# Long convolutions and their filters by a transform folded in time and in frequency, on eight shared 128x128 blocks

## The chip, the cores and the metric

One core of a Trainium2 chip runs the whole program. The metric is the device time of one execution in microseconds (us), as the median of several runs; lower is better. The core has five engines with a queue of instructions each: TensorE (PE, matrix products; its weight loads are listed as PEld), VectorE (DVE), ScalarE (ACT), GpSimd (POOL) and SyncE (SP), which here only issues transfers. An engine takes its instructions in order and waits on semaphores of the others.

## The reference

Two encoder layers on x of 512 times and 1024 channels. Each layer norms x, multiplies by one wide matrix `w_in`, and feeds two branches: differential attention with four heads, and a Hyena branch. In the Hyena branch three streams of 512 channels go through a short convolution of three taps. Then come two long convolutions, each with its own filter of 512 forward and 511 backward taps that a small network computes from the position, and each followed by a product with a gate:

```python
z = fft_long_conv(hv, filt[:, 0], flt_bias[l, 0]) * hx1
z = fft_long_conv(z, filt[:, 1], flt_bias[l, 1]) * hx2
y_h = z * silu(z_h)
def fft_long_conv(u, h_f, bias):            # n = 1024, cut to the first 512 times
    return irfft(rfft(u, n=2 * L) * h_f, n=2 * L)[:, :L] + u * bias
```

Both branches are gated by sigmoids, projected by `w_pa` and `w_ph`, added, projected by `w_out`, normed and added to x. All of it is float32.

## The kernel before, in words

Every float32 product is made of three: each operand is split into a high and a low part (`split`: a copy on ScalarE gives hi, a subtraction on VectorE gives lo), and `mm3` (line 180) accumulates hi*hi, hi*lo and lo*hi. The weights come through three buffers `wraw`, 256 KB a load, each split into `whi` and `wlo`.

The transform of 1024 points is cut into four groups of frequencies. `conv_in` turns a stream so that time is on the partition, adds and subtracts the four tiles of 128 times, and splits eight inputs. `conv_group` (one call for each of four groups) makes the real and imaginary part of a group from two inputs, 12 products 256 wide in all, multiplies by the filter's spectrum H that is read from DRAM, and splits the result. `conv_out` (one call for each of two tiles of 128 channels) goes back to time with the data as the stationary operand, 24 products 256 wide a call, so that its result has the channel on the partition, undoes the additions, and multiplies by the gate. A layer has four such convolutions: two filters (o) by two halves of 256 channels (hc). The filters themselves go through the same forward blocks in `filter_group`, eight calls for each of the eight filters of the program; the spectra are stored to DRAM.

The four constant tables `fh`, `fl`, `ih`, `il` hold 13 blocks of 128x128 each and are loaded by GpSimd's queue early in the program.

The order of the program is written as lists of steps that `mix` spreads evenly over each other, and a scheduler orders each engine's queue from it; `ahead(n)` lets a method's instructions rank n places earlier. In `layer`, after the attention, there are three such mixes around the long convolutions: the first convolution of half 0 with the rest of the Hyena projections, the first convolution of half 1 with three steps of `merge_a` (the gate and projection of the attention branch, 36 products 512 wide each), and the second convolution of both halves with the other five steps of `merge_a`. Then come eight steps of `merge_h`, in layer 0 mixed with three filters of layer 1, and the output projection. The eight `merge_a` steps of a layer each end in one instruction on VectorE at line 797, so these mark the stretch of the convolutions in the trace.

Of the kernel before, what the change touches and what calls it, by code (L numbers as in the profile page):

```python
# [17 lines left out]
P = 128  # L18
# [5 lines left out]
# tiles of each tag: how many, values a partition  # L24
TILES = {"hT": (8, 1024), "ya": (8, 512), "yh": (4, 1024), "s1": (12, 512), "s2": (4, 1024), "u": (12, 512),
         "ld": (2, 1024), "wraw": (3, 512), "whi": (4, 512), "wlo": (4, 512), "za": (2, 512), "a": (4, 512), "b": (3, 512)}
C8 = math.sqrt(0.5)
# [11 lines left out]
# ---------------------------------------------------------------- constants of the shapes  # L39
# [9 lines left out]

def _dft_matrices():  # L50
    p = np.arange(P, dtype=np.float64)[:, None]
    k = np.arange(P, dtype=np.float64)[None, :]
    th = 2 * np.pi * ((4 * k * p) % NF) / NF
    ph = [2 * np.pi * (((8 * k + r) * p) % NF) / NF for r in range(4)]
    sg = 1.0 - 2.0 * (k % 2)
    ny = (1.0 - 2.0 * (p % 2)) * np.ones((1, P))
    c, s = np.cos, np.sin

    def nyq(m):
        m = m.copy()  # L60
        m[:, 0] = ny[:, 0]
        return m

    fw = [c(th), sg * c(th), nyq(-s(th)), nyq(-sg * s(th)),
          c(ph[2]), -s(ph[2]), -c(ph[2]),
          c(ph[1]), -s(ph[1]), -c(ph[1]),
          c(ph[3]), s(ph[3]), -s(ph[3])]
    fw = np.stack(fw, 1)

    w = 2.0 / NF  # L70
    thT, sgT = th.T, sg.T
    e_re = w * c(thT)
    o_re = w * sgT * c(thT)
    e_im = -w * s(thT)
    o_im = -w * sgT * s(thT)
    e_re[0] = o_re[0] = 1.0 / NF
    e_im[0] = o_im[0] = ny[:, 0] / NF

    iv = [e_re, o_re, e_im, o_im, w * c(ph[2].T), -w * s(ph[2].T), -w * c(ph[2].T)]
    for r in (1, 3):  # L80
        iv += [-w * s(ph[r].T), w * c(ph[r].T), w * s(ph[r].T)]
    iv = np.stack(iv, 1)
    return fw, iv


def _constants():
    out = {}
    fw, iv = _dft_matrices()
    out["c_fh"], out["c_fl"] = _hi_lo(fw)
    out["c_ih"], out["c_il"] = _hi_lo(iv)  # L90
# [11 lines left out]
    ang = ((f32(2 * math.pi) * i[:, None]) * f[None, :] / f32(S)).astype(np.float64)  # L102
    out["c_z"] = np.ascontiguousarray(
        np.concatenate([t[None, :].astype(np.float64), np.cos(ang).T, -np.sin(ang).T], 0).astype(f32))
    p = np.arange(P)[:, None]
    out["c_nt"] = np.ascontiguousarray(
        np.concatenate([-t.reshape(4, P).T, np.where(p == 0, -1e30, 0.0), p > 0], 1).astype(f32))
    return out


# blocks of the forward matrices: per group the (re, im) pairs for its two inputs
FW = (((0, 1), (2, 3)), ((4, 5), (5, 6)), ((7, 8), (8, 9)), ((10, 11), (12, 10)))
# first of the two adjacent blocks of the inverse matrices for re and im
IV = ((0, 2), (4, 5), (8, 7), (11, 10))
# inputs of the groups among the slots [g, e, d, s, a1, b1, a3, b3]
SLOTS = ((1, 3), (0, 2), (4, 5), (6, 7))
# [14 lines left out]
def ahead(n):  # L131
    """the scheduler ranks the instructions of the method n places before (after, if negative) their place in the program"""
# [8 lines left out]
# ---------------------------------------------------------------- the kernel  # L141
class Net:
# [9 lines left out]
    # ---- tiles: the tiles of one tag are given out in the order of the program, so each stream has its own  # L152
    def t(self, tag, dt=F32, a=None):
        t = self.pools[tag].tile([P, TILES[tag][1]], dt, name=tag, tag=tag)
        return t if a is None else t.rearrange("p (a c) -> p a c", a=a)

# [10 lines left out]
    # ---- pieces  # L167
# [6 lines left out]
    def mm3(self, out, pairs):  # L174
        """out = sum of lhs.T @ rhs in float32, each operand given as (hi, lo)"""
# [6 lines left out]

    def split(self, hi, lo, src):
# [3 lines left out]
    def weights(self, src, to=None):  # L187
        """src: [128 k, c] of a matrix in DRAM, 512 values a partition -> (hi, lo), each [128, k, c]"""
# [8 lines left out]
    def rstd(self, ss, n, mul, eps, tag):  # L197
        """(ss * mul + eps) ** -0.5 of [128, n]"""
# [7 lines left out]
    def gain(self, src):  # L206
        g = [self.t("s1") for _ in range(2)]
# [4 lines left out]
    # ---- constants  # L212
# [9 lines left out]
    def load_dft(self):  # L222
        nc, a = self.nc, self.a
        self.fh = self.const([P, 13, P], "fh", F32R)
        self.fl = self.const([P, 13, P], "fl", F32R)
        self.ih = self.const([P, 13, P], "ih", F32R)
        self.il = self.const([P, 13, P], "il", F32R)
        for t, n in ((self.fh, "c_fh"), (self.fl, "c_fl"), (self.ih, "c_ih"), (self.il, "c_il")):
            self.tc.keep_in_program_order(nc.gpsimd.dma_start(out=t, in_=a[n]))

    def vectors(self):
        """the vectors over channels, channel on the partition: one transpose for each layer"""
        nc, a = self.nc, self.a
        self.nt = self.const([P, 6], "nt")
# [16 lines left out]
    def lambdas(self):  # L251
        """-lam of each layer, on every partition"""
# [22 lines left out]
    def bias_table(self):  # L275
        """tab[h, j] = -bias of head h at relative position j - 512"""
# [34 lines left out]
    def filter_mlp(self):  # L311
# [15 lines left out]
        # (hi, lo) of one layer, or (lo, hi), stacked along the contraction  # L327
# [10 lines left out]
        self.H = [[self.dram.tile([P, 2, 9, 256], F32, name=f"H{l}{o}", tag=f"H{l}{o}") for o in range(2)]  # L338
                  for l in range(DEPTH)]

    def filter_steps(self, l, blocks, where):
        """steps that fill H[l]; where: the phase that they run in, which has its own tiles to spare"""
        steps, late = [], []

        def group(*args):
            """the products of a group follow the splits of the next"""
            self.filter_split(*args[-3:])
            late.append(args)
            if len(late) > 1:
                self.filter_group(*late.pop(0))  # L350

        for o, hc in blocks:
            st = {"where": where}
            steps.append(lambda o=o, hc=hc, st=st: self.filter_load(l, o, hc, st))
            steps += [lambda o=o, t=t, st=st: self.filter_taps(l, t, st) for t in range(4)]
            for im in range(2):
                steps.append(lambda im=im, st=st: self.filter_sums(l, im, st))
                steps += [lambda o=o, hc=hc, im=im, g=g, st=st: group(l, o, hc, im, g, st) for g in range(4)]
        if blocks:
            steps.append(lambda: self.filter_group(*late.pop(0)))  # L360
        return steps

    def two(self, st):
        """two [128, 2, 256]"""
# [24 lines left out]
    def filter_taps(self, l, t, st):  # L389
        """sum and difference of the two directions at the times of tile t"""  # L390
# [6 lines left out]
        if t:  # L397
            nc.scalar.activation(out=h, in_=st["dl"], func=AF.Exp, scale=self.nt[:, t:t + 1])
        else:
            # the backward taps have none at time 0  # L400
            for d in range(2):
                nc.scalar.activation(out=h[:, d], in_=st["dl"][:, d], func=AF.Exp, scale=self.nt[:, 0:1],
                                     bias=self.nt[:, 4:5] if d else 0.0)
        nc.vector.tensor_tensor(out=h, in0=ps, in1=h, op=ALU.mult)
        if t == 0:
# [4 lines left out]
    def filter_sums(self, l, im, st):  # L410
        """st["T"][im] = (x0, x1), (x2, x3) -> (e, s), (g, d)"""
        x = st["T"][im]
        st["y"] = self.two(st)
        for y, op in zip(st["y"], (ALU.add, ALU.subtract)):
            self.nc.vector.tensor_tensor(out=y, in0=x[0], in1=x[1], op=op)

    @ahead(60)
    def filter_split(self, im, g, st):
        """the inputs of group g"""
        nc = self.nc  # L420
        es, gd = st["y"]
        if g < 2:
            src = (es, gd)[g]
        else:
            src = self.t("b", a=2)
            for j, y in enumerate((gd, es)):
                nc.vector.scalar_tensor_tensor(out=src[:, j], in0=y[:, 1], scalar=(C8 if g == 2 else -C8),
                                               in1=st["T"][im][j][:, 0], op0=ALU.mult, op1=ALU.add)
# [5 lines left out]
        self.split(yh, yl, src)  # L434
        st["in", im, g] = yh, yl

    def filter_group(self, l, o, hc, im, g, st):
        nc = self.nc
        yh, yl = st.pop(("in", im, g))
        ps = self.ps("po", 2)  # L440
        m = FW[g][im]
# [553 lines left out]
```

## Time and profile before

| what | value |
|---|---|
| time, median of 3 runs | 1008.47 us (1007.25 to 1008.93) |
| profiled execution: span | 1008.5 us |
| PE busy | 974.7 us (97%), 5619 matmuls |
| PEld busy | 847.6 us (84%) |
| DVE busy | 763.2 us (76%), 1599 instructions |
| ACT busy | 505.8 us (50%), 1035 instructions |
| POOL busy | 32.7 us (3%) |
| moved by DMA | 114.12 MB |

The profiled execution is one of the program on the chip; its span is the time from its first to its last instruction and differs from the median of the runs by less than 0.1 us. Busy times are unions over an engine's instructions; an engine's instructions overlap one another at their ends, so the distance from one start to the next is shorter than one instruction's duration.

### The profile page before, as it was taken

Reading aid. Unit: us, or ns where it says so; the run is one execution under the profiler, and the core shown is the slowest. Engines: PE = TensorE matmul, PEld = TensorE weight load, DVE = VectorE, ACT = ScalarE, POOL = GpSimd, SP = SyncE. Lnnn points to the kernel's source line nnn. Section 1 sums busy time; section 2 is a strip of 40 time slices with the busy share of each in tenths; the row PEclk is TensorE's granted clock in tenths of the full one; section 3 lists DMA queues with packets and bytes.
Section 4 is the critical chain, followed back from the end, with each engine's and each line's share of the span. In section 5 each row is a group of like instructions: output and inputs, shape, how many; then the busy total and the mean of one; then the engine's idle time right before and its main releaser. Section 6 shows DMA issues by size and latency. Waiting matters only on the chain.

```text
span 1008.5 us, 15608 instructions
## 1 busy us (share of the span) xinstructions
PE 974.7 (97%) x5619; PEld 847.6 (84%) x5619; DVE 763.2 (76%) x1599; ACT 505.8 (50%) x1035; POOL 32.7 (3%) x52
## 2 busy tenths in 40 slices
PE   3999999999999999999999999999999999999997
PEld 2878888888888888877899888888888888888887
DVE  3889889889689987977847586687778898864533
ACT  3477576555444434655645465565433543433421
POOL 2000000000000000000002000000000000000000
PEclk9999999999999999999999999999999999999999
DMA  8441432435334324334545233233332233523422
GB/s 286 124 132 51 140 99 85 130 84 145 115 95 117 111 75 135 104 95 131 181 123 185 82 91 93 84 89 95 106 109 84 82 116 111 176 75 94 134 76 84
DMA packets 150514, 114.12 MB, mean 113 GB/s; under 512 B 7634, under 2 KB 138336, under 8 KB 150437
## 3 DMA queue, kind: packets, MB, share of 16 engines
q1 hardware_dynamic: 149573, 109.20, 36.3%
q0 software_dynamic: 864, 3.93, 1.1%
q8 instruction: 44, 0.72, 0.3%
q14 instruction: 33, 0.27, 0.1%
HBM read 99.17 MB, written 13.93 MB: 112 GB/s over the span
## 4 chain that ended last, share of the span: by engine, by line
PE 81%; DMA 7%; DVE 4%; issue 4%; ACT 2%; POOL 1%; SPq 0%; DVEq 0%; POOLq 0%; ACTq 0%
PE pd L180 59%; PE po L180 10%; PE pq L180 5%; DMA wraw<-in_w_out 3%; PE pq L589 3%; PE pq L395 2%; DMA u<-in_flt_deltas 1%; PE pt L608 1%; DMA wraw<-in_w_in 1%; DMA yh<-in_x 1%; PE pt L703 1%; POOL ro L640 1%; DVE u L185 1%; DMA yh<-in_flt_deltas 0%; DVE wlo L185 0%
## 5 line engine op out<-in xcount | busy, mean ns | idle before, releaser
L180 PE MATMUL pd<-hT,whi 128*128 128x512 f32 x1408 | 455.8, 394 | 0.0
L180 PEld LDWEIGHTS pd<-hT,whi 128*128 128x128 f32 x1408 | 259.9, 188 | 49.7 <-PE pt L285 0.9
L180 PE MATMUL pd<-hT,wlo 128*128 128x512 f32 x704 | 277.2, 394 | 0.0
L184 ACT CAST whi<-wraw 128x512 fp32r<-128x512 f32 x228 | 140.9, 620 | 225.4 <-PE pd L180 171.4
L185 DVE TENSOR_TENSOR wlo<-wraw,whi 128x512 fp32r<-128x512 f32 x228 | 155.0, 685 | 74.8 <-ACT whi L184 73.4
L180 PEld LDWEIGHTS pd<-hT,wlo 128*128 128x128 f32 x704 | 132.4, 188 | 26.3 <-issue 0.2
L594 ACT ACTIVATE a<-a,m 128x512 f32<-128x512 f32 x64 | 46.1, 721 | 21.2 <-DVE m L592 20.7
L180 PE MATMUL pq<-s,fh 128*128 128x256 f32 x256 | 54.8, 283 | 0.0
L180 PE MATMUL po<-ih,s 128*128 128x256 f32 x256 | 50.0, 285 | 0.6 <-DVE b L759 0.6
L180 PE MATMUL pd<-whi,hT 128*128 128x256 f32 x192 | 40.2, 304 | 8.4 <-ACT whi L184 8.4
L589 PE MATMUL pq<-s,s 128*128 128x512 f32 x128 | 47.2, 399 | 0.2
L180 PEld LDWEIGHTS pq<-s,fh 128*128 128x128 f32 x256 | 42.7, 188 | 3.6 <-ACT s L184 1.3
L592 DVE CUSTOM_DVE_ANT_0 a<-pq,ld 128x512 f32<-128x512 f32 x64 | 43.3, 685 | 3.2 <-PE pq L589 2.6
L180 PEld LDWEIGHTS po<-ih,s 128*128 128x128 f32 x256 | 41.1, 188 | 1.7 <-ACT b L754 0.9
L180 PEld LDWEIGHTS pd<-whi,hT 128*128 128x128 f32 x192 | 33.1, 207 | 9.2 <-ACT whi L184 9.0
L180 PE MATMUL pd<-ya,whi 128*128 128x512 f32 x128 | 40.3, 390 | 0.0
L180 PE MATMUL pd<-yh,whi 128*128 128x512 f32 x128 | 40.2, 390 | 0.0
L184 ACT CAST s<-a 128x512 fp32r<-128x512 f32 x40 | 24.8, 619 | 28.4 <-DVE a L737 24.8
L180 PE MATMUL po<-il,s 128*128 128x256 f32 x128 | 36.1, 282 | 0.0
L180 PE MATMUL po<-u,fh 128*128 128x256 f32 x160 | 34.5, 287 | 0.9 <-ACT u L184 0.9
L180 PE MATMUL pq<-s,fl 128*128 128x256 f32 x128 | 34.1, 280 | 0.0
L832 DVE TENSOR_TENSOR yh<-pd,s 128x256 f32<-128x256 f32 x32 | 13.2, 421 | 27.5 <-ACT a L830 26.8
(219 smaller groups left out, 1839.1 us busy)
## 6 DMA issues: line engine op xcount, KB each, us to landing
wraw<-in_w_in SPq DMA_DIRECT2D x192, 256.0 KB
wraw<-in_w_out SPq DMA_DIRECT2D x32, 256.0 KB
H<-b SPq DMA_DIRECT2D x56, 128.0 KB
ld<-H SPq DMA_DIRECT2D x24, 256.0 KB
wraw<-in_w_pa SPq DMA_DIRECT2D x16, 256.0 KB
wraw<-in_w_ph SPq DMA_DIRECT2D x16, 256.0 KB
ld<-tab SPq DMA_DIRECT2D x8, 448.0 KB
ld<-H SPq DMA_DIRECT2D x8, 384.0 KB
```

The costliest lines, as they stand in the source:

```text
L180: self.nc.tensor.matmul(out, lhsT=l, rhs=r, start=(i == 0), stop=(i == n - 1))
L184: self.nc.scalar.copy(out=hi, in_=src)
L185: self.nc.vector.tensor_tensor(out=lo, in0=src, in1=hi.bitcast(F32), op=ALU.subtract)
L395: nc.tensor.matmul(ps[:, d], lhsT=self.a3[:, t * P:(t + 1) * P], rhs=w[:, d], start=(n == 0), stop=(n == 1))
L589: nc.tensor.matmul(ps, lhsT=st["q"][c][:, tsl], rhs=st["k"][c][n], start=(n == 0), stop=(n == 1))
L592: nc.vector.tensor_tensor_reduce(out=lg, in0=ps, in1=st["B"][:, 384 - i * P:896 - i * P], scale=1.0, scalar=3e38, op0=ALU.add, op1=ALU.min ...
L594: nc.scalar.activation(out=lg, in_=lg, func=AF.Exp, scale=-1.0, bias=m, accum_out=(s0, s1)[c])
L608: nc.tensor.transpose(out=ps[:, k], in_=w[:, k * P:(k + 1) * P], identity=self.ident)
L640: nc.gpsimd.tensor_tensor(out=r, in0=m, in1=self.nhalf, op=ALU.pow)
L703: nc.tensor.transpose(out=ps[:, k], in_=u[0][ct][:, k * P:(k + 1) * P], identity=self.ident)
L832: nc.vector.tensor_tensor(out=st["o"][tt][:, cs], in0=ps, in1=g, op=ALU.mult)
```

## The change

The transform is folded both in time and in frequency, about time 256. Times of one parity before and after the middle are added and subtracted (`conv_fold`), and even and odd times (E, O) go to even and odd frequencies (E, O) by eight blocks, `CEE` to `COO` for cosines and `SEE` to `SOO` for sines. The same blocks serve the way there, the way back and the filters; `ih` and `il` are gone. Five more blocks of whole numbers (`XA`, `XB` and so on), with no low part, carry the frequencies that fold onto themselves. There are two calls of `conv_group` a convolution instead of four, each over 1024 values a partition. `conv_out` is now one call, with the blocks as the stationary operand, so its result has time on the partition. Between the two convolutions of a half the result stays like that: `conv_gate` turns the gate instead of the data. Only the second result is turned back to channels on the partition (`conv_last`). The first two streams are kept in an order of their own (`short_conv` writes them in two pieces, the second half backwards), and are read in steps of two when they are turned.

```diff
-TILES = {..., "s1": (12, 512), ..., "u": (12, 512), "ld": (2, 1024), ..., "a": (4, 512), "b": (3, 512)}
+TILES = {..., "s1": (6, 1024), ..., "u": (12, 514), "ld": (2, 1024), "hb": (1, 512), "cx": (3, 1024), ...,
+         "a": (4, 514), "b": (3, 512)}
...
+    def dft_sum(self, out, terms):
+        ops = []
+        for n, hi, lo in terms:
+            bh, bl = self.dft[n]
+            ops += [(bh, hi), (bl, hi), (bh, lo)] if n not in EXACT[1:] and n != "SE2" else [(bh, hi), (bh, lo)]
+            if n == "SE2":
+                ops.append((self.dft["SEE"][1], hi))
+        for i, (b, y) in enumerate(ops):
+            self.nc.tensor.matmul(out, lhsT=b, rhs=y, start=(i == 0), stop=(i == len(ops) - 1))
...
-        for t, n in ((self.fh, "c_fh"), (self.fl, "c_fl"), (self.ih, "c_ih"), (self.il, "c_il")):
+        for t, n in ((fh, "c_fh"), (fl, "c_fl")):
...
     def filter_group(...):            # 2 calls for im = 0, 2 for im = 1, instead of 4 and 4
-        self.mm3(ps[:, 0], [(self.fh[:, m[j]], self.fl[:, m[j]], yh[:, j], yl[:, j]) for j in range(2)])
+        even = [(c + "E" + f, yh[:, 0], yl[:, 0])]
+        if im == 0:
+            even.append((("FA", "FB")[ft], zh[:, 0], zl[:, 0]))
+        self.dft_sum(ps[:, 0], even)
+        self.dft_sum(ps[:, 1], [(c + "O" + f, yh[:, 1], yl[:, 1])])
+        nc.scalar.activation(out=odd, in_=ps[:, 1], func=AF.Copy, scale=s)
+        for j, op in ((0, ALU.add), (1, ALU.subtract)):
+            nc.vector.scalar_tensor_tensor(out=hs[:, j], in0=ps[:, 0], scalar=s, in1=odd, op0=ALU.mult, op1=op)
...
+    def turned(self, u, ct, ps):      # conv_in, conv_gate
+        for half in range(2):
+            for j in range(2):
+                t = slice(256 * (1 - half) + j, 256 * (2 - half), 2)
+                self.nc.tensor.transpose(out=ps[half][:, j, ct * P:(ct + 1) * P], in_=u[:, t], identity=self.ident)
...
     def conv_group(self, l, o, hc, st, ft):
+        for j, t in enumerate("EO"):
+            re = [("C" + t + f, yh[:, j], yl[:, j])]
+            im = [("S" + t + f, yh[:, 2 + j], yl[:, 2 + j])]
+            if t == f == "E":
+                re.append(("XA", yh[:, 2], yl[:, 2]))
+                im.append(("XB", yh[:, 0], yl[:, 0]))
+            self.dft_sum(U[j][:, 0], re)
+            self.dft_sum(U[j][:, 1], im)
+        nc.scalar.copy(out=odd, in_=U[1])
+        for s, op in ((0, ALU.add), (1, ALU.subtract)):
+            nc.vector.tensor_tensor(out=X[:, 2 * s:2 * s + 2], in0=U[0], in1=odd, op=op)
+        nc.vector.tensor_tensor(out=four(W), in0=four(X), in1=both(B), op=ALU.mult)
+        nc.vector.tensor_tensor(out=four(X), in0=four(X), in1=both(A) if ft else four(first), op=ALU.mult)
+        nc.vector.tensor_tensor(out=X[:, 0:4:2], in0=X[:, 0:4:2], in1=W[:, 1:4:2], op=ALU.subtract)
+        nc.vector.tensor_tensor(out=X[:, 1:4:2], in0=X[:, 1:4:2], in1=W[:, 0:4:2], op=ALU.add)
+        for s, op in ((0, ALU.add), (1, ALU.subtract)):
+            nc.vector.tensor_tensor(out=W[:, 2 * s:2 * s + 2], in0=X[:, 0:2], in1=X[:, 2:4], op=op)
+        self.split(*st["Q", f], W)
+    def conv_out(self, st):
+        self.dft_sum(c[:, 0], [("CEE", *q("E", 0)), ("COE", *q("O", 0)), ("XA", *q("E", 1))])
+        self.dft_sum(c[:, 1], [("CEO", *q("E", 2)), ("COO", *q("O", 2))])
+        self.dft_sum(s[:, 0], [("SE2", *q("E", 1)), ("SOE", *q("O", 1)), ("XB2", *q("E", 0))])
+        self.dft_sum(s[:, 1], [("SEO", *q("E", 3)), ("SOO", *q("O", 3))])
+        nc.scalar.copy(out=sines, in_=s)          # then 4 additions and subtractions 256 wide give y
+    def conv_last(self, hc, u, st, ct):
+        for j in range(4):
+            nc.tensor.transpose(out=ps[:, j], in_=y[:, j, cs], identity=self.ident)
...
-        mix(self.conv_steps(l, 0, 0, u0), hy0[4:5] + tail[3:4] + hy0[5:6] + tail[4:] + hy0[6:] + hy1, second[:n1])
-        mix(self.conv_steps(l, 0, 1, u1), ma[:3], second[n1:])
-        mix(self.conv_steps(l, 1, 0, u0) + self.conv_steps(l, 1, 1, u1), ma[3:])
+        c0, c1 = self.conv_steps(l, 0, u0), self.conv_steps(l, 1, u1)
+        mix(c0[0], hy0[4:5] + tail[3:4] + hy0[5:6] + tail[4:] + hy0[6:] + hy1, second[:n1])
+        mix(c1[0], ma[:3], second[n1:])
+        mix(c0[1] + c1[1], ma[3:])
```

Two places show how the queues move. The first is PE's queue in the third mix of layer 0, where the first of the two halves is finished. Before, `conv_out` of that half takes the split results (`s_...`) of the four groups in turn as the stationary operand, against the constants `ih` and `il`, and nothing of the half follows on PE:

```order
L180 MATMUL po<-ih,s_3465 128x256 [waits DVE_49,Activation_49]
L180 MATMUL po<-il,s_3465 128x256
L180 MATMUL po<-ih,s_3466 128x256
L180 MATMUL po<-ih,s_3465 128x256
L180 MATMUL po<-il,s_3465 128x256
L180 MATMUL po<-ih,s_3466 128x256
L180 MATMUL po<-ih,s_3522 128x256
```

After, the last products of `conv_out` (`po`) are followed by the transposes of `conv_last` (`pt<-ident,cx`), which wait for VectorE's additions on that very result, with one product of the next gate (`pd<-hT,whi`) ahead of them:

```order
L204 MATMUL po<-s_3648,fl 128x256
L204 MATMUL po<-s_3649,fh 128x256
L192 MATMUL pd<-hT,whi 128x512 [waits Activation_49]
L867 MATMUL pt<-ident,cx 128x128 [waits DVE_49]
L867 MATMUL pt<-ident,cx 128x128
L192 MATMUL pd<-hT,whi 128x512
L867 MATMUL pt<-ident,cx 128x128 [waits DVE_49]
```

What moved is the turn from time to channels: it was part of the products, and is now a step of its own behind a round over ScalarE and VectorE.

The second place is VectorE's queue for one group in the third mix of layer 0. Before, a group took five instructions, of 512 and 256 values: the two products with H (lines 734 and 735, from PE's result `pq` and the load of H, `ld`), two sums (736, 737) and the low part of the split at line 185 (`s_4323`), which PE waits for; the other rows in between split inputs and weights:

```order
L734 TENSOR_TENSOR a<-pq,ld 128x512
L185 TENSOR_TENSOR s_4292<-s_4258,s_4291 128x512
L735 TENSOR_TENSOR a<-pq,ld 128x512
L185 TENSOR_TENSOR wlo<-wraw,whi 128x512
L736 TENSOR_TENSOR a<-a 128x256
L737 TENSOR_TENSOR a<-a 128x256
L185 TENSOR_TENSOR s_4323<-a,s_4322 128x512
```

After, a group takes nine, of 512 and 1024 values: `cx` are the group's own tiles, `ld` and `hb` the parts of H, and line 208 with `s_3868` is the low part of the split that PE waits for:

```order
L821 TENSOR_TENSOR cx<-pq,a 128x512 x2
L824 TENSOR_TENSOR cx<-cx,hb 128x1024
L825 TENSOR_TENSOR cx<-cx,ld 128x1024
L821 TENSOR_TENSOR cx<-pq,a 128x512 x2
L826 TENSOR_TENSOR cx<-cx 128x2x256
L827 TENSOR_TENSOR cx<-cx 128x2x256
L899 SCALAR_TENSOR_TENSOR u<-a,pd 128x512
L830 TENSOR_TENSOR cx<-cx 128x512 x2
L208 TENSOR_TENSOR wlo<-wraw,whi 128x512
L824 TENSOR_TENSOR cx<-cx,ld 128x1024
L208 TENSOR_TENSOR s_3868<-cx,s_3867 128x1024
```

What moved is that one chain of longer instructions stands where two shorter ones of two groups stood, with the start of the other group (the second pair at line 821, and 824 with `ld` alone) and a gate's end (line 899) put in between.

## Rows read from the trace of the kernel before

**Rows 1.** Page, part 1: busy time, share of the span, instructions.

```profile
PE 974.7 (97%) x5619; PEld 847.6 (84%) x5619; DVE 763.2 (76%) x1599; ACT 505.8 (50%) x1035; POOL 32.7 (3%) x52
```

**Rows 2.** Windows by stage: busy time of each engine, granted clock, DMA share, GB/s.

```profile
core 0: us, PE busy (x) PEld busy (x) DVE busy (x) ACT busy (x) POOL busy (x), PEclk, DMA share, GB/s
188.00:298.00 110.00, 109.26 (x595) 93.22 (x595) 90.92 (x181) 54.24 (x105) 1.98 (x2) 1.00 0.38 110
298.00:392.00 94.00, 94.00 (x560) 82.97 (x559) 84.54 (x189) 42.00 (x82) 0.00 (x0) 1.00 0.39 116
392.00:492.00 100.00, 96.83 (x523) 81.50 (x522) 83.67 (x166) 58.31 (x117) 0.00 (x0) 0.98 0.37 108
788.00:881.00 93.00, 93.00 (x550) 82.06 (x549) 83.00 (x185) 39.91 (x77) 0.00 (x0) 1.00 0.41 121
```

**Rows 3.** Chain that ended last: start, length in us, what.

```profile
318.77 2.71 PE po L180 x23
...
887.11 58.28 PE pd L180 x257
```

**Rows 4.** Timeline of PE, transposes and the product after them.

```profile
16.30 1.05 PE L484 MATMUL pt<-ident,s 128*128 128x128 f32 x4
17.01 0.77 PE L180 MATMUL pd<-whi,hT 128*128 128x256 f32 x2
...
105.51 0.60 PE L608 MATMUL pt<-ident,a 128*128 128x128 f32 x4
105.87 0.48 PE L180 MATMUL pd<-hT,wlo 128*128 128x512 f32 x1
```

**Rows 5.** Timeline of DVE: the first and eighth `merge_a` end of layer 0.

```profile
297.70 0.68 DVE L797 SCALAR_TENSOR_TENSOR u<-a,pd 128x512 f32<-128x512 f32 x1
...
391.70 0.69 DVE L797 SCALAR_TENSOR_TENSOR u<-a,pd 128x512 f32<-128x512 f32 x1 [1.62 <-PE pd L180]
```

**Rows 6.** Windows, 890 to 945 us (columns as in rows 2).

```profile
890.00:945.00 55.00, 55.00 (x245) 45.53 (x244) 26.92 (x42) 19.50 (x34) 0.00 (x0) 1.00 0.33 96
```

**Rows 7.** Groups by line and form: busy us, mean ns, idle before.

```profile
L180 PE MATMUL pq<-s,fh 128*128 128x256 f32 x256 | 54.8, 283 | 0.0
L180 PE MATMUL po<-ih,s 128*128 128x256 f32 x256 | 50.0, 285 | 0.6 <-DVE b L759 0.6
...
L868 DVE SCALAR_TENSOR_TENSOR ld<-yh,rout,ld 128x1024 f32<-128x1024 f32 x4 | 5.1, 1284 | 2.1 <-POOL rout L203 2.1
...
L764 DVE SCALAR_TENSOR_TENSOR a<-b,a 128x256 f32<-128x256 f32 x16 | 6.7, 416 | 0.0
...
L783 ACT ACTIVATE a<-pd 128x512 f32<-128x512 f32 x32 | 19.0, 593 | 1.9 <-PE pd L180 1.8
```

**Rows 8.** Timeline of DVE, instructions back to back.

```profile
327.00 0.28 DVE L762 TENSOR_TENSOR b<-b 128x128 f32<-128x128 f32 x1
327.21 0.68 DVE L185 TENSOR_TENSOR yh<-b,yh 128x512 fp32r<-128x512 f32 x1
327.81 0.42 DVE L763 TENSOR_TENSOR a<-a,b 128x256 f32<-128x256 f32 x1
328.14 0.42 DVE L764 SCALAR_TENSOR_TENSOR a<-b,a 128x256 f32<-128x256 f32 x1
328.48 0.68 DVE L185 TENSOR_TENSOR wlo<-wraw,whi 128x512 fp32r<-128x512 f32 x1
```

**Rows 9.** DMA issues, KB each, median us from issue to landing.

```profile
fh<-in_c_fh POOLq DMA_DIRECT2D x1, 832.0 KB, 5.0
...
il<-in_c_il POOLq DMA_DIRECT2D x1, 832.0 KB, 10.7
```

**Rows 10.** POOL's timeline, the chain, and PE's timeline, at the start.

```profile
13.67 0.71 POOL L229 DMA_DIRECT2D fh<-in_c_fh  x1
...
15.45 0.54 POOL L229 DMA_DIRECT2D il<-in_c_il  x1
...
14.61 9.22 DMA wraw<-in_w_in
...
24.53 0.79 PE L180 MATMUL pd<-whi,hT 128*128 128x256 f32 x2 [4.75 <-ACT whi L184]
```

More of the change, by code (lines that the diff above doesn't have):

```diff
@@ L47, in _hi_lo @@
     return np.ascontiguousarray(hi), np.ascontiguousarray(_round12(x - hi.astype(np.float64)))
+BLOCKS = ("CEE", "CEO", "COE", "COO", "SEE", "SEO", "SOE", "SOO")
+EXACT = ("SE2", "XA", "XB", "XB2", "FA", "FB")
 def _dft_matrices():
[L51 to L76, printed above, removed]
@@ L206, in gain @@
     def gain(self, src):
-        g = [self.t("s1") for _ in range(2)]
+        g = self.two_of("s1")
         for j in range(2):
@@ L343, in filter_steps, with split, taps @@
         steps, late = [], []
[L345 to L350, printed above, removed]
+        def split(im, j, st):
+            self.filter_split(im, j, st)
+            if late:
+                late.pop(0)()
+        def taps(o, t, st):
+            self.filter_taps(l, t, st)
+            if late:
+                late.pop(0)()
         for o, hc in blocks:
@@ L545, in q @@
             ps = self.proj(l, QC + h * P)
-            st["q"] = [self.t("s1", F32R) for _ in range(2)]
+            st["q"] = self.two_of("s1", F32R)
             for c in range(2):
@@ L691, in conv_steps @@
+    def conv_steps(self, l, hc, u):
+        st = {}
         return ([lambda ct=ct: self.conv_in(u, st, ct) for ct in range(2)]
-                + [lambda g=g: self.conv_group(l, o, hc, st, g) for g in range(4)]
-                + [lambda ct=ct: self.conv_out(l, o, hc, u, st, ct) for ct in range(2)])
+                + [lambda ft=ft: self.conv_group(l, 0, hc, st, ft) for ft in range(2)]
+                + [lambda: self.conv_out(st), lambda: self.conv_gate(u, st)],
+                [lambda ft=ft: self.conv_group(l, 1, hc, st, ft) for ft in range(2)]
+                + [lambda: self.conv_out(st)] + [lambda ct=ct: self.conv_last(hc, u, st, ct) for ct in range(2)])
@@ new lines, in turned, with conv_fold @@
+    def turned(self, u, ct, ps):
+        for half in range(2):
+            for j in range(2):
+                t = slice(256 * (1 - half) + j, 256 * (2 - half), 2)
+                self.nc.tensor.transpose(out=ps[half][:, j, ct * P:(ct + 1) * P], in_=u[:, t], identity=self.ident)
+    def conv_fold(self, st, late, early):
+        nc = self.nc
+        pm = self.t("cx", a=4)
+        mask = self.nt[:, NT_MASK:NT_MASK + 1]
+        self.fold(pm[:, 0:2], late, early, NT_MASK, ALU.add)
+        nc.vector.scalar_tensor_tensor(out=pm[:, 2], in0=late[:, 0], scalar=mask, in1=early[:, 0], op0=ALU.mult, op1=ALU.subtract)
+        nc.vector.tensor_tensor(out=pm[:, 3], in0=late[:, 1], in1=early[:, 1], op=ALU.subtract)
+        st["Y"] = self.t("s1", F32R, 4), self.t("s1", F32R, 4)
+        self.split(*st["Y"], pm)
@@ new lines, in conv_in, with conv_group @@
+        if ct == 0:
+            st["ps"] = [self.ps("pt", 2) for _ in range(2)]
+        self.turned(u[0][ct], ct, st["ps"])
+        if ct == 1:
+            early = self.t("a", a=2)
+            self.nc.scalar.copy(out=early, in_=st["ps"][1])
+            self.conv_fold(st, st["ps"][0], early)
+    @ahead(30)
+    def conv_group(self, l, o, hc, st, ft):
+        nc = self.nc
+        H = self.H[l][o][:, hc]
+        first, b = self.t("ld", a=4), None
+        if ft:
+            self.load(first, H[:, 6:10])
+            A, B = first[:, 0:2], first[:, 2:4]
+        else:
+            B = self.t("hb", a=2)
+            self.load(first, H[:, 0:4])
+            self.load(B, H[:, 4:6])
+        yh, yl = st["Y"]
+        f = "EO"[ft]
+        U = [self.ps("pq", 2) for _ in range(2)]
+        for j, t in enumerate("EO"):
[6 more added lines that the diff above has]
+            self.dft_sum(U[j][:, 1], im)
+        odd = self.t("a", a=2)
+        nc.scalar.copy(out=odd, in_=U[1])
+        X, W = self.t("cx", a=4), self.t("cx", a=4)
+        for s, op in ((0, ALU.add), (1, ALU.subtract)):
+            nc.vector.tensor_tensor(out=X[:, 2 * s:2 * s + 2], in0=U[0], in1=odd, op=op)
+        four = lambda t: t.rearrange("p (s c) x -> p s c x", s=2)
+        both = lambda t: t.rearrange("p (s c) x -> p s c x", c=1).broadcast_to([P, 2, 2, 256])
+        nc.vector.tensor_tensor(out=four(W), in0=four(X), in1=both(B), op=ALU.mult)
[4 more added lines that the diff above has]
+            nc.vector.tensor_tensor(out=W[:, 2 * s:2 * s + 2], in0=X[:, 0:2], in1=X[:, 2:4], op=op)
+        st["Q", f] = self.t("s1", F32R, 4), self.t("s1", F32R, 4)
+        self.split(*st["Q", f], W)
```

295 lines of the change are left out of this document (147 added, 148 removed).

## The prediction

> **What bounds the kernel now.** I read the page's busy shares first. PE stands at 97% and VectorE at 76% [rows 1], which names PE but does not prove it, since the matmul records overlap. So I looked for the distance from one product to the next in a dense piece of the chain. There 23 products 256 wide take 2.71 us, 0.118 us each, and 257 products 512 wide take 58.28 us, 0.227 us each [rows 3]; the mean durations of 283 to 285 ns in the groups [rows 7] are more than twice the first of these and price nothing. A transpose costs 0.09 us (four in 0.36 us until the next product starts) [rows 4].
>
> With these prices I counted the order of PE between the first and the eighth `merge_a` step of layer 0: 252 products 512 wide, 292 products 256 wide and 16 transposes make 57.2 + 34.5 + 1.4 = 93.1 us. The trace takes 391.70 - 297.70 = 94.0 us for it [rows 5]. PE is therefore full there, to 1%. VectorE is busy for 84.5 of those 94 us [rows 2], so it is close behind, and the reader should see in the same rows that it is as close (83.0 of 93) in layer 1, but not elsewhere.
>
> The Trainium skill (Perfetto Trace Analysis, Identifying the Most-Contended Engine) warns that matmul busy share is a poor measure and asks for the share of weight loads instead. That share is 84% here [rows 1], which by that rule would leave 16% open. The trace disagrees for this mix: from 890 to 945 us, where products follow each other without a gap, the weight loads also stand at 45.53 of 55 us, 83% [rows 6].
>
> **What the change does, part by part.** *Products.* Counting both orders, a convolution's `conv_group` goes from 48 products 256 wide to 28 and its `conv_out` from 48 to 28; with eight convolutions that is 320 fewer. A filter goes from 52 to 28; with eight filters, 192 fewer. Together 512 x 0.118 = **-60.4 us** of PE. The 512-wide ones stay. Transposes grow by 32 (`conv_last`; those of `conv_gate` replace a `conv_in`): 32 x 0.09 = **+2.9 us**. 64 transposes now read every second value, which no row shows. I price them as the plain ones; at 0.18 us, the slowest quartet of the trace (0.71 us to the next product) [rows 4], they would add 5.7 us, and I see no reason for a gain.
>
> *VectorE.* Back to back, 128 values take 0.21 us, 256 take 0.33 and 512 take 0.60 [rows 8]. An instruction of 1024 values is new in these stretches; continuing the line gives 0.60 + 2 x 0.27 = 1.13 us, and the 1284 ns of the only 1024-wide group [rows 7] is the upper bound. I take 1.13, because the durations of the others exceed their distances by 0.08 us or more as well. In the stretch above, VectorE had 82.6 us by these prices and now has 71 x 0.60 + 19 x 1.13 + 30 x 0.33 and a little = 75 us, while PE has 252 x 0.227 + 196 x 0.118 + 18 x 0.09 = 81.9 us. VectorE's share of PE's work rises only from 89% to 91%. Over the program it loses some 29 us and ScalarE some 36 us; neither counts while PE is full.
>
> *New waits.* The long chain of a group puts results later against PE's queue, so I compared the two queues in the third mix of layer 0. From the end of `conv_out` of the preceding half to the low part of the last split of the next `conv_out`, VectorE has 21 instructions of 512 values, 7 of 1024 and 12 of 256: 12.6 + 7.9 + 4.0 = 24.5 us. Ahead of it stands the end of the last product (0.28) and ScalarE's copy (0.59) [rows 7]: 25.4 us. PE has 72 products 512 wide and 55 products 256 wide until it wants that result, 22.8 us. So it waits 2.6 us. Then the transposes of `conv_last` wait for 0.28 + 0.59 + 0.42 (first sum, line 764's form [rows 7]), covered by one product of 0.23: 1.1 us more. The other half has more products in between and waits for nothing by the same count. What is queued behind the waiting instructions is the gate's product, so the whole of it counts. Layer 1 has the same order: 2 x 3.7 = **+7.4 us**. The bounds are 0, if the 1.13 is too much by a little and hi parts come early, and double, if VectorE is held at two more places of the four convolutions.
>
> *Where PE is not alone.* In the attention of layer 0 two filters run; PE loses 5 us there but VectorE, busy beside it, only 4: I give back 1 us. Beside `merge_h` of layer 0, PE has 288 x 0.227 + 234 x 0.118 = 93.0 us and the stretch takes 100 [rows 2]: 7 us already go to the filters' own chain of loads, sums and stores. PE loses 114 products there, 13.5 us, and the chain gets shorter in instructions but not in steps; I give back 2 us. Together **+3 us**.
>
> *The constants.* Four tables of 832 KB become two of 896 and 512 KB, 1.9 MB less. GpSimd issues them from 13.67 to 15.99 us, around the weight load that is issued at 14.61, lands 9.22 us later, and leaves PE idle for 4.75 us [rows 10]; the first table lands in 5.0 us, the last in 10.7 [rows 9]. With the last two gone I take **-3 us**; the bounds are 0 and 4.75.
>
> *Covered at no cost.* GpSimd's eight copies of one value stand between steps of an engine that is 3% busy [rows 1], and `conv_last` needs them tens of microseconds later; uncovered they would cost about what its rows have, 0.54 to 0.71 us each [rows 10]. H is read in pieces of 512 KB, where it was 256; the load is issued one group ahead, and VectorE has 7 us of work a group. SyncE's queue holds weight loads behind these; if a load of H held them, the next gate would be late by up to the 12 x 0.227 = 2.7 us that the products of one load take.
>
> **Sum.** The profiled execution has 1008.5 us, the median of the runs to within 0.1. 1008.5 - 60.4 + 2.9 + 7.4 + 3 - 3 = **958.4 us**.
>
> **Rivals.** *VectorE and its chains take over the convolutions.* For it: 84.5 of 94 us before. Against it: its work falls there too. PE's gain in the three mixes is 7 and 11 us in layer 0 and 6 and 10 in layer 1, 34 in all. If none of it comes through, the time is 1008.5 - (57.5 - 34) + 3 - 3 = 985.
>
> *Slower.* Each of eight convolutions now has a group's chain of some 7 us twice (6 x 0.60 + 3 x 1.13 each) and a `conv_out` of one piece, where eight shorter calls used to overlap. If PE stood exposed to more than 57.5 / 8 = 7.2 us of it at each, about half of the 14, the kernel would be slower; at 10 us each it is 1008.5 - 57.5 + 80 = 1031. Against it: the count above finds 3.7 us for two convolutions.
>
> *PE has room, so that nothing comes back.* The removed products fall into the 16% of the span in which no weights are loaded [rows 1], 161 us, and the time stays at 1008. Against it stand the 93.1 us of work in 94.0 us [rows 5] and the 83% of the gapless stretch [rows 6]. It is what the rule of the Trainium skill (Perfetto Trace Analysis, Identifying the Most-Contended Engine) would give here.
>
> *No new waits and the whole of the start.* 1008.5 - 57.5 - 4.75 = 946, for which VectorE only has to be a little ahead of my prices.
>
> **Numbers.** A run of this kernel tells a change from none at about 0.2%, 2 us. Forecast as worked out, 948 to 970: 0.68. No new waits, 948 or less: 0.11. VectorE takes over, 970 to 995: 0.15. Nothing comes back: 0.02. Slower: 0.04. So faster 0.94, same 0.02, slower 0.04. The range runs from 946 to 976: below by the bound without waits, above by doubled waits (7.4) and slow transposes (5.7) and no gain at the start (3); it leaves out some 0.2. The time predicted is that of the likeliest.
>
> **What will show it.** The products of the transform should be 672 by count at 0.118 us apart, and transposes of `u` at 0.09. From the first to the eighth `merge_a` end, layer 0 should take 86 us instead of 94, with VectorE busy for 75 to 78. PE should wait for line 208 and for the sums behind `conv_out`, some 4 us a layer, and at the start for less than 2 us at the weights. If the stretch stays above 92 us, VectorE or its chain has taken over; if PE's waits are in the filters instead, my +3 is the step that failed; if a 1024-wide instruction takes 1.28 us apart, the chain was mis-sized. A transpose at 0.18 would be the step of the strides.

## The result, and the profile after

The changed kernel takes 1061.49 us, the median of 4 runs (1059.54 to 1063.84), against 1007.88 us (1007.25 to 1008.93) before: 1.052 times as long, with a 95% interval of 1.0492 to 1.0548. The forecast was 958.4 us, and its range ended at 976. The span of the profiled execution is 1057.8 us.

The page's busy shares, to be read beside [rows 1]:

```profile
PE 943.8 (89%) x5139; PEld 807.5 (76%) x5139; DVE 735.7 (70%) x1439; ACT 468.0 (44%) x927; POOL 42.0 (4%) x58
```

PE has 480 instructions fewer, as counted (512 products less, 32 transposes more), and yet its share fell from 97% to 89%. So it waits, and the next question is for what. Three timelines of one such place, those of PE, DVE and SP (start, length, what; in brackets the idle time before it and what ended it):

```profile
122.21 2.93 PE L192 MATMUL po<-s,yh 128*128 128x256 f32 x12 [9.99 <-DVE b L489]
```
```profile
121.40 0.76 DVE L489 SCALAR_TENSOR_TENSOR b<-po,b 128x256 f32<-128x256 f32 x2 [10.58 <-DMA H<-b]
```
```profile
106.38 0.74 SPq L184 DMA_DIRECT2D H<-b  x2
107.59 8.38 SPq L181 DMA_DIRECT2D ld<-tab  x1
116.08 2.93 SPq L181 DMA_DIRECT2D wraw<-in_w_in  x3
```

PE waits for VectorE, VectorE waits to overwrite a `b` that a store to H is still reading, and SyncE's next load, issued behind that store, takes 8.38 us to issue. The windows around it:

```profile
core 0: us, PE busy (x) PEld busy (x) DVE busy (x) ACT busy (x) POOL busy (x), PEclk, DMA share, GB/s
107.00:111.00 4.00, 4.00 (x37) 4.00 (x36) 3.82 (x9) 2.88 (x8) 0.52 (x2) 1.00 0.29 84
111.00:114.00 3.00, 1.23 (x11) 1.02 (x9) 0.00 (x0) 0.37 (x1) 0.00 (x0) 1.00 0.07 24
114.00:122.00 8.00, 0.00 (x0) 0.00 (x0) 0.60 (x2) 0.00 (x0) 0.00 (x0) 0.69 0.58 170
122.00:126.00 4.00, 3.79 (x17) 3.79 (x18) 1.16 (x4) 0.25 (x1) 0.00 (x0) 0.50 0.21 78
```

From 111 to 114 us the core's 16 DMA engines are busy for 0.07, about one of them, and move 24 GB/s. When PE starts again, its granted clock is 0.50, the lower of the two levels, 1.2 GHz; it had stood idle for 9.99 us. The DMA issues name the store:

```profile
H<-b SPq DMA_DIRECT2D x32, 256.0 KB
...
H<-b SPq DMA_DIRECT2D x8, 254.0 KB
...
H<-b SPq DMA_DIRECT2D x8, 2.0 KB
```

Eight of them carry 254 KB: 127 rows, one for each filter, the `self.store(H[1:P, 1:4:2], hs[1:P])` of `filter_group`. At 24 GB/s one would take 10.8 us. The eight waits (122.21, 203.49, 294.95, 363.14, 467.32, 507.85, 544.64 and 873.35 us) are 9.1 to 10.8 us long. Five groups of PE's waits hold them (in all, times, longest), whatever engine they name:

```profile
PE po L204 <- ACT a L844: 30.3, 3, 10.8
PE pq L426 <- ACT za L207: 20.3, 2, 10.2
PE po L204 <- DVE b L489: 11.1, 2, 10.4
PE pd L192 <- DVE hT L208: 10.5, 2, 9.6
PE po L192 <- DVE b L489: 10.0, 1, 10.0
```

The Trainium skill (DMA: Bandwidth & Descriptors, Why a DMA increments its semaphore by 16 and not by 1) says that a transfer runs on the largest number of engines, 16 at most, that divides the slowest dimension of both sides, and names 127 partitions as a case of one engine. By that rule the store has one engine, and the trace agrees with its 0.07.

At the start PE begins with 2.23 us of waiting instead of 4.75, and 3.0 us earlier than in [rows 10]:

```profile
21.52 0.79 PE L192 MATMUL pd<-whi,hT 128*128 128x256 f32 x2 [2.23 <-ACT whi L207]
```

### The profile page after: what moved, and what is told of

Same layout as the page of the kernel before. It is cut to its first block, busy times and chain, and to the rows that moved or that the text cites. A ratio compares the mean times of both kernels' runs of the same rounds, so it can differ in the third digit from the quotient of the medians.

```text
span 1057.8 us, 14325 instructions
## 1 busy us (share of the span) xinstructions
PE 943.8 (89%) x5139; PEld 807.5 (76%) x5139; DVE 735.7 (70%) x1439; ACT 468.0 (44%) x927; POOL 42.0 (4%) x58
## 5 line engine op out<-in xcount | busy, mean ns | idle before, releaser
L192 PE MATMUL pd<-hT,whi 128*128 128x512 f32 x1408 | 465.9, 403 | 2.6 <-ACT a L885 2.6
L426 PE MATMUL pq<-za,a 128*128 128x256 f32 x96 | 24.9, 307 | 20.3 <-ACT za L207 20.3
L204 PE MATMUL po<-yh,fh 128*128 128x256 f32 x60 | 14.2, 323 | 30.3 <-ACT a L844 30.3
L720 DVE SCALAR_TENSOR_TENSOR u<-pd,vec,u 128x256 f32<-128x256 f32 (+2 forms) x80 | 39.4, 531 | 1.7 <-ACT u L718 1.3
L192 PE MATMUL po<-s,yh 128*128 128x256 f32 x192 | 30.0, 294 | 10.4 <-DVE b L489 10.0
L192 PE MATMUL pd<-hT,s 128*128 128x256 f32 x192 | 28.4, 297 | 9.8 <-DVE hT L208 9.6
L192 PEld LDWEIGHTS po<-s,yh 128*128 128x128 f32 x192 | 27.3, 198 | 12.8 <-DVE b L489 10.2
L426 PEld LDWEIGHTS pq<-za,a 128*128 128x128 f32 x96 | 19.1, 214 | 22.4 <-ACT za L207 21.0
L204 PEld LDWEIGHTS po<-yh,fh 128*128 128x128 f32 x60 | 11.4, 223 | 31.6 <-ACT a L844 31.2
L204 PE MATMUL pq<-s,fh 128*128 128x256 f32 x160 | 35.1, 293 | 0.0
```

Of the source, the lines that this page charges most:

```text
L192: self.nc.tensor.matmul(out, lhsT=l, rhs=r, start=(i == 0), stop=(i == n - 1))
L204: self.nc.tensor.matmul(out, lhsT=b, rhs=y, start=(i == 0), stop=(i == len(ops) - 1))
L426: nc.tensor.matmul(ps[:, d], lhsT=self.a3[:, t * P:(t + 1) * P], rhs=w[:, d], start=(n == 0), stop=(n == 1))
L720: nc.vector.scalar_tensor_tensor(out=o, in0=src, scalar=w[j], in1=o, op0=ALU.mult, op1=ALU.add)
```

## The experiments

**First question: the stores.** Theory A: the store of 127 rows on one DMA engine is the loss. Theory B: VectorE and the chains of the groups, as the rivals of the prediction had it. Theory C: the buffers `b` wait for any store of H. In the first kernel (called so from here on) the store takes all 128 rows; row 0 of these two slots is overwritten by the later store of one row, as in the changed kernel, so H ends with the same values:

```
-            self.store(H[1:P, 1:4:2], hs[1:P])
+            self.store(H[:, 1:4:2], hs)
```

> The store of the odd slots of H covers 128 rows instead of rows 1 to 127 (row 0 is overwritten by the later store of one row, as before). Theory A (a store of 127 rows runs on one of the sixteen DMA engines, about 10 us, and holds every transfer queued behind it; eight such stores): the eight waits of about 10 us on PE vanish with the low clock behind them, and the time is 955 to 965 us. Theory B (VectorE and the long group chains hold PE, the store is only where it shows): the time stays above 1040 us. Theory C (the buffers b wait for any store to land, whatever its rows): above 1040 us too, with the waits for the landing of H still there.

Measured: 970.72 us (967.27 to 971.74), 0.9612 of before (0.9576 to 0.9649), so 90.8 us less than the changed kernel. The page:

```profile
PE 929.7 (96%) x5139; PEld 794.6 (82%) x5139; DVE 734.4 (76%) x1439; ACT 468.3 (48%) x927; POOL 42.0 (4%) x58
```

The eight waits sum to 80.7 us. With them PE's busy time for the same 5139 matmuls falls from 943.8 to 929.7 us, as it would where PE no longer restarts at a clock of 0.50; no run tells this part of the price from the waits. A holds, though 970.72 lies over its 955 to 965. Now as two stores, of 112 and of 15 rows, with the same bytes as the changed kernel's:

```
-            self.store(H[1:P, 1:4:2], hs[1:P])
+            self.store(H[1:113, 1:4:2], hs[1:113])
+            self.store(H[113:P, 1:4:2], hs[113:P])
```

> The 127 rows are stored by two transfers, of 112 rows (7 x 16) and of 15 rows. Theory A: 112 rows spread over the sixteen engines, 15 rows are at worst an eighth of the old store on one engine (some 1.2 us), so 955 to 970 us, although there is one store more. Theory C: at least the 1061 us of the changed kernel, since there is one landing more to wait for.

Measured: 971.8 us in one run, 1.8 over the range. Row 0 is not what matters, and one store more costs nothing that can be seen. Next, the kernel before gets the fault: its store of two slots is split into row 0 and rows 1 to 127.

```
+        if n == 2:
+            self.store(self.H[l][o][0:1, hc, 0:2], hs[0:1, :2])
+            self.store(self.H[l][o][1:P, hc, 0:2], hs[1:P, :2])
+        else:
-        self.store(self.H[l][o][:, hc, first:first + n], hs[:, :n])
+            self.store(self.H[l][o][:, hc, first:first + n], hs[:, :n])
```

> The kernel before, with the 256 KB store of each filter's first two slots cut into row 0 and rows 1 to 127 (the same values). Theory A: eight new waits of some 10 us each, 60 to 110 us more than before, 1070 to 1120 us, with one of sixteen DMA engines busy (a share of 0.06 to 0.08) during each. Theories B and C: within 10 us of before, 1008 to 1018 us.

Measured: 1069.94 us in one run, 60.4 more than before on that chip (1009.51) and at the lower edge of A's range. PE shows seven new waits of 3 us or more and not eight of 10: 8.51, 7.00, 3.70, 3.02, 8.82, 8.81 and 8.62 us, 48.5 in all. They come with the store, without anything else of the change; why they are fewer and shorter than expected was not followed up. One of them:

```profile
461.20 0.58 PE L180 MATMUL po<-u,fh 128*128 128x256 f32 x1 [8.82 <-ACT u L184]
```

Last, half of the bytes: of the two slots one is stored over 128 rows, the other over 127.

```
-            self.store(H[1:P, 1:4:2], hs[1:P])
+            self.store(H[:, 1], hs[:, 0])
+            self.store(H[1:P, 3], hs[1:P, 1])
```

> The changed kernel with half of the store spread: slot 1 as 128 rows of 1 KB, slot 3 as 127 rows of 1 KB. Theory A: the lone engine has half the bytes, so each of the eight waits falls from some 10 us to some 4 or 5 us or less, and the time lies about half way, 990 to 1015 us. If the cost were per transfer and not per byte on the lone engine, it would stay near 1061 us.

Measured: 1010.71 us in one run, 40.0 above the first kernel where the whole store is 90.8 above it. The wait at the place shown above is 5.20 us instead of 9.99:

```profile
115.73 0.58 PE L192 MATMUL po<-s,yh 128*128 128x256 f32 x1 [5.20 <-DVE b L489]
```

The price goes with the bytes on that engine, a little under half for half of them. B and C would have left it where it was.

**Second question: 12 us too many.** With the stores mended the kernel still missed 958.4. The chain of the first kernel (start, length, what) shows where:

```profile
698.38 15.16 PE pd L192 x65
...
847.93 60.24 PE pd L192 x257
```

These are 0.2332 and 0.2344 us for a product 512 wide, against 0.2268 in [rows 3]; the instructions read alike in both programs, and the granted clock is 1.00 in both. The new shapes of the tiles do move the tiles: `hT` starts at byte 46,304 of each partition before and at 30,976 after, `whi` at 191,712 and at 191,104. So theory D was the place in SBUF, and theory E anything else. Four kernels, three with an unused constant in `setup` ahead of all tiles (32 or 64 bytes), one with `hb` longer by 32 bytes and the weights behind it:

```
+        nc.vector.memset(self.const([P, 8], "gap"), 0.0)
...
-TILES = {... "hb": (1, 512), ...}
+TILES = {... "hb": (1, 520), ...}
```

> The changed kernel with the stores of H over all 128 rows, and an unused constant of 32 bytes a partition ahead of all pools, so that every tile behind it starts 32 bytes later. Without the constant (970.7 us) the 512-wide products stood 0.2332 us apart, in the kernel before 0.227. Theory D (the place of the operands in SBUF: the streamed tiles start at a multiple of 64 bytes in the changed kernel and 32 bytes past one in the kernel before): 512-wide products 0.227 us apart again, 2,624 x 0.0064 = 16.8 us less, so 954 us (950 to 960). Theory E (another thing of the changed kernel, such as what the other engines and transfers do beside it): still 0.233 apart and 970 us.

> The same with 64 bytes instead of 32, as a control. Theory D with a period of 64 bytes: 0.233 us apart and 970 us. If merely being moved counted, or a period of 128 bytes or more, it would differ from 970 us by several us. Theory E: 970 us.

> The kernel before with the unused 32 bytes, which puts its streamed tiles on multiples of 64 bytes. Theory D: its 512-wide products go from 0.227 to 0.233 us apart, 2,624 x 0.0064 = 16.8 us more, so 1024 us (1020 to 1028). Theory E: unchanged, 1008 us.

> The changed kernel with the stores of H over all 128 rows, where the one tile hb is 32 bytes longer: the tiles behind it, the weights whi and wlo among them, start 32 bytes later, while hT, ya, yh and s1, which the 512-wide products stream, stay on multiples of 64 bytes. Theory D with the streamed operand as what counts: 0.233 us apart and 970 us. Theory D with the loaded operand as what counts: 0.227 us and 954 us. Theory E: 970 us.

Measured: 973.03 (971.28 to 975.66), 971.44 (970.32 to 973.8), 1006.95 (1004.31 to 1008.43; 0.9981 of before, 0.9968 to 0.9993) and 971.21 us (969.9 to 972.17). No 512-wide product changed its pace; the first and the third read

```profile
847.36 60.24 PE pd L192 x257
```
```profile
881.65 58.29 PE pd L180 x257
```

so the start address over 64 bytes, the form of D that I had in mind, falls, and E had forecast as much. D was left with coarser forms. Two kernels put `hb` and `cx` ahead of `hT`, and `u` behind `wlo`, the first with 992 unused bytes more:

```
-TILES = {"hT": (8, 1024), ... "u": (12, 514), "ld": ..., "hb": ..., "cx": ..., "wraw": ..., "whi": ..., "wlo": ..., ...}
+TILES = {"hb": ..., "cx": ..., "hT": (8, 1024), ... "ld": ..., "wraw": ..., "whi": ..., "wlo": ..., "u": (12, 514), ...}
```

> The changed kernel with the stores of H over all 128 rows, its tiles placed in another order behind an unused constant of 992 bytes, so that hT, ya, yh, s1 and s2 (all that the 512-wide products stream) start at exactly the addresses of the kernel before, and whi and wlo at a distance from them that differs from before's by a multiple of 2,048 bytes. Theory D (the place in SBUF, in any form: absolute, or of one operand against the other): 512-wide products 0.227 us apart and 954 us (950 to 960). Theory E (not the place in SBUF): 0.233 apart and 971 us.

> The same order without the unused constant: the streamed tiles 992 bytes lower, the distance to the weights as in q1. Theory D in the form of the distance between streamed and loaded operand: 0.227 us apart, 954 us. Theory D in the form of the absolute address, and theory E: 0.233 apart and 971 us.

Measured: 964.54 us (963.88 to 965.66) and 961.64 us (959.3 to 965.66), 0.9556 and 0.9529 of before, over the 950 to 960 of D. The pace is back in both, so E falls; that of the second:

```profile
843.35 58.60 PE pd L192 x257
```

As the second kernel's streamed tiles do not lie where they lay before, their absolute address falls too. Two forms were tried next: the distance between the streamed and the loaded tile (F), or whether the streamed tiles lie low or high (G). One kernel keeps all streamed tiles where the pace was 0.233 and moves the weights by 128 bytes; the other keeps the order that gave 0.228 and moves the weights 384 bytes off:

```
+TILES = {... "hb": (1, 544), ...}
...
+TILES = {"cx": ..., "hT": ..., ... "s2": ..., "hb": (1, 608), "ld": ..., ... "wlo": ..., "u": ..., ...}
```

> The changed kernel with the stores of H over all 128 rows and the old order of tiles, where the tile hb is 128 bytes longer: hT, ya, yh and s1 stay at the addresses at which the 512-wide products stood 0.233 us apart, and whi and wlo come to a multiple of 512 bytes from them (160,256 bytes from hT to whi; in the changed kernel 160,128, in the kernel before 145,408 = 284 x 512). Theory F (the distance between the streamed and the loaded tile, by its remainder over 512 bytes): 0.227 to 0.228 us apart, and 958 to 965 us. Theory G (where the streamed tiles lie in SBUF, low or high): 0.233 apart and 971 us.

> The order of tiles of the run at 961.6 us, with hb, 384 bytes longer, between the streamed tiles and the weights: the streamed tiles move 2,048 bytes, and whi comes to 123,264 bytes from hT, 384 over a multiple of 512 as in the changed kernel. Theory F: the 512-wide products back at 0.233 us apart, 2,624 x 0.006 = 15 us less what the clock takes, so 969 to 976 us. Theory G: 0.227 apart and 962 us.

Measured: 962.28 us (961.46 to 963.39), 0.9543 of before (0.9526 to 0.956), and 969.16 us (966.62 to 973.86), 0.9626 (0.9596 to 0.9657). Their chains:

```profile
694.24 14.78 PE pd L192 x65
842.08 58.56 PE pd L192 x257
```
```profile
694.92 15.16 PE pd L192 x65
844.34 60.00 PE pd L192 x257
```

The first is at 0.2274 to 0.2279, the second at 0.2332 to 0.2335. G falls, and all kernels go as F has it. In the table, "over 512" is the remainder after division by 512, and a product's time is that of the chain's 257 products; the medians are from three chips, on which the kernel before took 1008.53 to 1009.51.

| kernel | hT to whi, bytes | over 512 | start of whi, over 512 | a product, us | median, us |
|---|---|---|---|---|---|
| before | 145,408 | 0 | 224 | 0.2268 | 1009.26 |
| before, 32 unused bytes | 145,408 | 0 | 256 | 0.2268 | 1006.95 |
| first kernel (128 rows) | 160,128 | 384 | 128 | 0.2344 | 970.72 |
| 32 unused bytes | 160,128 | 384 | 160 | 0.2344 | 973.03 |
| 64 unused bytes | 160,128 | 384 | 192 | 0.2344 | 971.44 |
| weights moved by 32 | 160,160 | 416 | 160 | 0.2344 | 971.21 |
| other order, 992 unused bytes | 120,832 | 0 | 224 | 0.2279 | 964.54 |
| other order | 120,832 | 0 | 256 | 0.2280 | 961.64 |
| weights moved by 128 | 160,256 | 0 | 256 | 0.2279 | 962.28 |
| other order, weights off | 123,264 | 384 | 128 | 0.2335 | 969.16 |

That the place in SBUF sets the pace is shown; that it is the distance is not. The start of `hT` alone is out: it is byte 30,976 in the first kernel and in the one with the weights moved by 128. The start of `whi` alone (`wlo` has the same remainder) is a rival that is left: 224 and 256 go with the fast pace and 128, 160 and 192 with the slow one, in every row, and no run parts it from F. The traces lean towards F, by little. Over all products of `hT` with `whi` or `wlo` that follow two of their kind, the mean distance in time is 0.2327 us in each of the four slow kernels with a remainder of 384, wherever `whi` starts, and 0.2335 in the one with 416, although its `whi` starts at the same byte as with 32 unused bytes.

## Why the prediction was wrong

The direction failed at the part "Covered at no cost". It follows H on its way back, "read in pieces of 512 KB", and SyncE's queue behind these reads; the stores of H are named once, in the filters' chain behind the +3, and have no term anywhere. The change splits one store for each filter into row 0 and 127 rows, and the second part, eight stores of 127 rows in all, costs 90.8 us in the runs (1061.49 - 970.72). The two rivals that end late, VectorE over the convolutions and PE exposed to a group's chain, are not what happened: each of the eight long waits stands behind a filter's store. The line "if PE's waits are in the filters instead, my +3 is the step that failed" pointed at the place, but the +3 was for a chain of steps with its waits, and the cause is one transfer on one DMA engine. (The upper bound of 976 does not come out of its own terms either: 958.4 + 7.4 + 5.7 + 3 is 974.5.)

With the stores over 128 rows the steps can be read one by one.

*The stretch of layer 0* from the first to the eighth `merge_a` end: 86 us forecast, VectorE at 75 to 78. In the first kernel (DVE's timeline, and the window):

```profile
294.10 0.68 DVE L899 SCALAR_TENSOR_TENSOR u<-a,pd 128x512 f32<-128x512 f32 x1
...
380.10 0.68 DVE L899 SCALAR_TENSOR_TENSOR u<-a,pd 128x512 f32<-128x512 f32 x1
```
```profile
294.10:380.10 86.00, 82.75 (x463) 70.48 (x462) 77.12 (x125) 31.99 (x52) 0.00 (x0) 1.00 0.43 129
```

By these marks it takes 86.0 us, where [rows 5] have 94.0. In the changed kernel the same stretch takes 97.4 (328.32 to 425.68), with one of the eight waits, that at 363.14, in it. That the 86 is met to the tenth is luck, for the marks slipped. PE's last products of the first and of the eighth step are, before and in the first kernel,

```profile
296.90 0.40 PE L180 MATMUL pd<-ya,wlo 128*128 128x512 f32 x1
...
391.21 0.39 PE L180 MATMUL pd<-ya,wlo 128*128 128x512 f32 x1
```
```profile
289.61 0.40 PE L192 MATMUL pd<-ya,wlo 128*128 128x512 f32 x1
...
377.89 0.48 PE L192 MATMUL pd<-ya,wlo 128*128 128x512 f32 x1
```

VectorE's first mark stood 0.4 us behind the end of its product and now stands 4.1 behind it. On PE the stretch went from 94.3 to 88.3 us, 2.3 more than forecast. Its 252, 196 and 18 instructions are as counted; 252 x 0.0064 = 1.6 us are slower 512-wide products, of which more below. VectorE's 1.13 us for 1024 values held: 1.14 from one start to the next (326.32 to 327.46).

*The new waits* were put at 3.7 us a layer. PE's timeline shows them where the count had them, in order the low part's wait and the sums' behind `conv_out`:

```profile
342.30 0.39 PE L204 MATMUL po<-s,fh 128*128 128x256 f32 x1 [0.93 <-ACT s L207]
343.57 0.72 PE L204 MATMUL po<-s,fh 128*128 128x256 f32 x4 [0.52 <-DVE s L208]
347.05 0.50 PE L192 MATMUL pd<-hT,whi 128*128 128x512 f32 x1 [1.17 <-ACT a L885]
```

That is 2.6 us (1.45 for 2.6, and 1.17 for 1.1), and the same in layer 1: 5.2 instead of 7.4. A wait of 0.53 us at 336.48, for the low part of a weight, was not in the count. *The start*: 3.0 us, as forecast.

*The transposes of every second value* were taken at 0.09 us. In the kernel at 962.28 us they alternate with products 256 wide, and four pairs take 313.33 - 312.33 = 1.00 us:

```profile
312.33 0.28 PE L769 MATMUL pt<-ident,u 128*128 128x128 f32 x1
312.36 0.37 PE L204 MATMUL pq<-s,fh 128*128 128x256 f32 x1
...
313.33 0.29 PE L769 MATMUL pt<-ident,u 128*128 128x128 f32 x1
```

Less 0.118 for the product, one costs 0.13, between my two bounds; over 64 that is 2.6 us more than the sum has. Whether the step of two or the alternation costs it was not tried.

*The +3 where PE is not alone* came out near in sum, and not in its parts. In the kernel at 962.28 us PE takes 282.0 us from its first transpose to the last product of the first `merge_a` step (7.87 to 289.83), where before it took 289.5 (7.43 to 296.90). That is 7.5 less, while 112 products 256 wide fewer, 8 transposes more and the start make 13.2 - 0.7 + 3.0 = 15.5. So 8 us were lost there, where the forecast gave back 1; waits of 1.79, 2.55 and 1.51 us stand at 125.24, 243.10 and 251.12. From the eighth step to the first transpose of layer 1 it takes 18.2 us less (379.15 to 501.26; before 391.21 to 531.54), while 120 products fewer and 6 transposes more make 13.6: over 4 us were gained where the forecast gave back 2.

*"The 512-wide ones stay"* is the term that was mis-sized among those that remain. They stay in number, but in the first kernel at 0.233 to 0.234 us each. Moving the weights by 128 bytes gives 970.72 - 962.28 = 8.4 us, half of the 16.8 that 2,624 products x 0.0064 make. The 0.0064 was read in long unbroken runs. Over all products of `hT` with `whi` or `wlo` that follow two of their kind, the mean distance falls from 0.2327 to 0.2280 us, and 2,624 x 0.0047 make 12.3, which still leaves 3.9. The gain comes late: shortly before the end of layer 0 the two kernels still stand only 0.4 us apart,

```profile
479.17 1.10 PE L192 MATMUL pd<-hT,ya 128*128 128x256 f32 x7 [1.11 <-DVE yh L933]
```
```profile
478.78 1.46 PE L192 MATMUL pd<-hT,ya 128*128 128x256 f32 x10 [0.91 <-DVE yh L933]
```

and the kernel with the better pace shows a lower granted clock in two places of that half, where the first kernel has 1.00:

```profile
120.00:136.00 16.00, 13.64 (x67) 10.77 (x65) 13.01 (x28) 11.02 (x24) 0.00 (x0) 0.89 0.45 136
344.00:352.00 8.00, 6.83 (x36) 6.05 (x36) 4.54 (x12) 2.10 (x4) 0.00 (x0) 0.79 0.27 74
```

But the first kernel has two such places too, where the other has 1.00:

```profile
20.00:28.00 8.00, 6.64 (x41) 6.44 (x42) 5.14 (x13) 3.37 (x10) 0.00 (x0) 0.79 0.62 130
488.00:496.00 8.00, 6.03 (x38) 5.96 (x38) 3.75 (x7) 3.22 (x10) 0.00 (x0) 0.79 0.45 136
```

Over the whole span the granted clock is 0.994 in the first kernel and 0.993 in the other, some 1 us, so the clock does not carry what is missing. Where the missing 3.9 are is open; no run was made for them.

With both causes taken out, the kernel takes 962.28 us, 3.9 above the forecast and inside its range. The counts of the products held. That the sum comes so near is in part luck, since the 8 us lost and the 4 gained around the filters, the slower transposes and the smaller waits offset each other. What the prediction left out is how the results leave the core, and where the tiles lie.

## What to carry to other kernels

Read the rows of every transfer that a change touches, not its bytes alone: cutting one row off a store of 128 made 127, and 2 KB less in each of eight stores cost 90.8 us; all 128 rows, or a split into 112 and 15, cost nothing that could be seen. A wait on such a store is named in the trace by the engine that wants the buffer back, two steps from PE, so follow the chain to the DMA. When tiles get another size or order, read the time from one product to the next anew, in products that did not change, before pricing them at the old rate.

## What the runs showed of the hardware

A store of 254 KB over 127 rows used one of 16 DMA engines (share 0.07, 24 GB/s), and PE waited 9.1 to 10.8 us for it; with half of the bytes 5.20 us at the same place.

A 512-wide product followed its predecessor after 0.227 to 0.228 us where the loaded tile `whi` lay a multiple of 512 bytes from the streamed tile `hT`, and after 0.233 to 0.234 us with a remainder of 384 or 416 bytes. In the same kernels the start of `whi` over 512 was 224 or 256 at the fast pace and 128, 160 or 192 at the slow one, so whether the distance counts or that start alone is not shown; the start of the streamed tile alone does not set it. Only these values were tried, for products 256 wide nothing was compared, and why the place counts is open.
